# Attention logits in a decoder block: keys of the heads in place of latent queries

## The chip, the cores and the metric

The kernel runs on one core of a Trainium2 chip. The metric is the time of one execution on the device, in microseconds; the median of three runs of the kernel before is 1537.74 (1536.7 to 1537.75). Engines are named as in the profile: PE (TensorE) multiplies matrices, DVE (VectorE) and ACT (ScalarE) work on vectors, POOL is GpSimd, SP issues most DMAs.

## What is computed

A decoder block on 512 tokens of width 1024, in f32: a mixer (sparse attention beside a pooling branch, gates, an output projection, LayerNorm) and a mixture of 32 experts with four per token. The change lies in the attention. Its keys are a latent of 128 numbers per token, shared by eight heads of width 64:

```python
q_lat = jnp.einsum('bshd,rhd->bshr', q, w_uk[l]) * (ATTN_HEAD_DIM ** -0.5)
ckv = rms_norm(ckv, kv_norm_g[l])
...
logits = jnp.einsum('bqhr,bqkr->bqhk', ql, c_sel).astype(jnp.float32)
logits = logits - slopes[None, None, :, None] * dist[:, :, None, :]
p = jax.nn.softmax(logits, axis=-1).astype(c_sel.dtype)
return jnp.einsum('bqhk,bqkr->bqhr', p, c_sel)
```

A query attends only to the 128 keys that an indexer scores highest among those up to its own position. The logit of a head is a product over r (128) and d (64) of query, up-projection `w_uk` and latent; it can be bracketed from either side.

## The kernel before, in words

The program is one stream per engine, in the order in which the Python code emits it; nothing reorders it. Queries stand in four blocks of 128, and block b sees (b+1)*128 keys. The latent is kept twice: `ckv`, tokens on partitions, and `ckvT` (line 724), its 128 numbers on partitions.

The projections come first, with weights split into two parts so that three fp32r products give f32 (`proj`, line 564): 24 matmuls of 512 columns each. A pair of split weights is made three projections ahead (`one_pair`, line 536): ACT copies the high part (504 or 542), DVE subtracts it (505 or 543). A raw weight tile is free after its last split, and SP then issues the next load of its ring of four. The q projection (lines 716 to 732) also turns the latent (723), and at its third step turns the up-projection `wuk` (728) into `wukT`, scaled (729).

Scores of the indexer (`score_pair`, line 634) and rounds that take the top eight keys (`top_round`, line 654) are queued and drained between the projections, by a cost that is a formula of the number of columns (`drain`, line 664). `score_pair` multiplies two heads at a time, one on partitions 0 to 63, one on 64 to 127.

The attention (lines 907 to 923) runs eight units, (block, half of the heads), in the order of blocks 3, 0, 2, 1. `queries(b)` (line 829) makes the queries of all eight heads of a block in the latent's coordinates, 128 rows by 128 queries each, from `wukT` and `qT`, and copies them out of PSUM with DVE and ACT (837). `logits(u)` (839) multiplies four heads by `ckvT`, a head to a PSUM bank, and DVE adds the distance and the mask (849). `exponentials(u)` (853) takes the maximum (DVE, 856) and exponentiates (ACT, 858). `weights(u)` (861) divides by the sums (DVE, 867). `outputs(u)` (869) transposes the weights (877), copies them by ACT and DVE in turn (878) and multiplies by `ckv` (884); `values(u)` (887) applies `w_uv` (892). The order is set by hand:

```python
weights(u - 1)
logits(u)
outputs(u - 1)
exponentials(u)
drain(STEP_BUDGET)
if u < 7:
    ga_tile(u)
values(u - 1)
```

`queries` comes ahead of these at the units 2, 4 and 6, and once before the loop; `ga_tile` is one more projection (ACT copies it out, line 820). PSUM has four banks of tag "a" (projections and logits), two of "b" (queries, outputs, values) and two of "c" (transposes). Tiles share named slots of SBUF: a tile in a slot waits for the last reader of the tile before. After the loop come the branch products (`branch_part`, line 780), the output projection, the first norm and the router (to line 1240), and then the experts, whose weights SP loads as slots come free (`Stream`, line 183; first load in line 1038).

Of the kernel before, what the change touches and what calls it, by code (L numbers as in the profile page):

```python
# [25 lines left out]
OP = mybir.AluOpType  # L26
AX = mybir.AxisListType

P = 128
S = 512  # L30
# [4 lines left out]
HD = 64  # L35
# [35 lines left out]
def tile_hybrid_block(ctx, tc, x, c, w_ada, b_ada, w_in, kv_norm_g, w_uk, w_uv, w_pool_group,  # L71
                      pool_scale, w_branch_attn, w_branch_pool, w_out, ln1_g, ln1_b, w_router,
                      b_router, w_gate_up, b_gate_up, w_down, b_down, ln2_g, ln2_b, out):
    nc = tc.nc
# [14 lines left out]
    def bank(tag, shape=None, dt=F32):  # L89
        bufs = {"a": 4, "b": 2, "c": 2}[tag]  # L90
        return psum.tile(shape or [P, 512], dt, name="ps_" + tag, tag=tag, bufs=bufs)
# [4 lines left out]
    def slot(shape, tag, dt=F32, bufs=1, name=None):  # L96
        pool = stream if tag in LASTING else ft_last if tag in LAST else ft
        return pool.tile(shape, dt, name=name or tag, tag=tag, bufs=bufs)
# [181 lines left out]
    bada = slot([12, 512], "bada")  # L280
# [59 lines left out]
    small = {}  # L340

    def small_loads(*rows):
        def load():
            for name, shape, tag, src in rows:
                small[name] = slot(shape, tag, name=name)
                nc.sync.dma_start(small[name], src)
        return load

    feed.add("small", small_loads(("kvg", [P, R], "kvg", kv_norm_g.to_broadcast([P, R])),
                                  ("wuk", [P, 512], "u", w_uk[0].rearrange("r h d -> r (h d)")),  # L350
                                  ("wpg", [P, 4, P], "wpg", w_pool_group[0].rearrange("g c d -> c g d"))),
             ring=False)
    add_cols(("q", 0), Q0)
# [19 lines left out]
    ident = consts.tile([P, P], F32, name="ident")  # L373
# [64 lines left out]
    ps = bank("c")  # L438
# [125 lines left out]
    def proj():  # L564

        w = next_pair()
        ps = bank("a")
        proj_part(ps, w, range(KD))
        return ps
# [43 lines left out]
    def ada_group():  # L613
        g = next(ada_groups)
        ps, w = bank("c"), [ada_feed.tiles["ada2", g, j] for j in range(2)]
        for j in range(2):
            for b in range(4):
                nc.tensor.matmul(ps[32 * b:32 * b + 32, :], condp[:, 2 * (g % 4) + j, :], w[j][:, b * 512:(b + 1) * 512],
                                 start=(j == 0), stop=(j == 1))
        part = w[1][:, 0:512]  # L620
        nc.scalar.copy(part, ps)
        nc.scalar.dma_start(mod_parts[g % 4, 4 * (g // 4):4 * (g // 4) + 4, :], part[::32])
        ada_feed.mark(("ada2", g))
# [40 lines left out]
    def drain(budget):  # L664
        cost = 0.0
        if pair_q:
            b, j = pair_q.pop(0)
            cost += score_pair(b, j)
            if j == 3:
                top_q.extend((b, r) for r in range(TOPK // 8))  # L670
        while top_q and cost < budget:
            cost += top_round(*top_q.pop(0))

    BUDGET, STEP_BUDGET = 3.6, 3.0
    kiT = slot([P, S], "kiT")
# [14 lines left out]
    ckvT = slot([P, S], "ckvT")  # L690
# [3 lines left out]
    ps = bank("b", [P, NT, H])  # L694
# [5 lines left out]
    def normal_ckv():  # L700
        ps = bank("c", [P, NT, R])
        for t in range(NT):
            nc.tensor.transpose(ps[:, t, :], ckvT[:, t * P:(t + 1) * P], ident)
        for t in range(NT):
            nc.scalar.activation(sq, ps[:, t, :], AF.Square, accum_out=ssum[:, t:t + 1])
        nc.vector.tensor_scalar(ssum, ssum, 1.0 / R, EPS, op0=OP.mult, op1=OP.add)
        nc.scalar.activation(ssum, ssum, AF.Sqrt)
        nc.vector.reciprocal(ssum, ssum)
        for t in range(NT):
            nc.vector.scalar_tensor_tensor(ckv[:, t, :], ps[:, t, :], ssum[:, t:t + 1], small["kvg"],  # L710
                                           op0=OP.mult, op1=OP.mult)


    qT = slot([P, 4, S], "C0", name="qT")
    wukT = slot([P, 4, P], "bada", name="wukT")
    for j in range(4):
        nc.scalar.copy(qT[:, j, :], proj())
        if j == 0:
            normal_ckv()
        if j == 1:  # L720
            ps = bank("c")
            for t in range(NT):
                nc.tensor.transpose(ps[:, t * P:(t + 1) * P], ckv[:, t, :], ident)
            nc.scalar.copy(ckvT, ps)
        if j == 2:
            ps = bank("c")
            for i in range(4):
                nc.tensor.transpose(ps[:, i * P:(i + 1) * P], small["wuk"][:, i * P:(i + 1) * P], ident)
            nc.scalar.mul(wukT, ps.rearrange("p (j r) -> p j r", j=4), HD ** -0.5)
        if j % 2:  # L730
            ada_group()
        drain(BUDGET)
# [35 lines left out]
    for g in range(4):  # L768
        ps = proj()
# [17 lines left out]
    def branch(w, i, v):  # L787
        ps = bank("a")
        branch_part(ps, w, i, v, range(4))
        return ps  # L790

    for g in range(4):
        for i in range(2):
            n = 2 * g + i
# [10 lines left out]
        for i in range(2):  # L805
            n = 2 * g + i
# [4 lines left out]
    def selected(b):  # L811

        while any(v[0] == b for v in pair_q + top_q):
            drain(0.1)
# [4 lines left out]
    def ga_tile(n):  # L819
        nc.scalar.copy(ga[n // 4][:, n % 4, :], proj())  # L820

    ya_raw = slot([P, 4, S], "C1", name="ya_raw")
    units_at = [(b, g) for b in (3, 0, 2, 1) for g in range(2)]
    ql = [slot([P, 4, P], tag, name="ql") for tag in ("kiT", "pooled")]
    pT = slot([P, 2, 512], "usum", name="pT")
    oT = slot([P, 2, 512], "relu", name="oT")
    state = {}

    def queries(b):

        qs = slice(b * P, (b + 1) * P)
        for i in range(2):
            hp = slice(i * HD, (i + 1) * HD)
            ps = bank("b", [P, 4, P])
            for j in range(4):
                nc.tensor.matmul(ps[:, j, :], wukT[hp, j, :], qT[hp, j, qs], start=True, stop=True)
            (nc.scalar.copy if i else nc.vector.tensor_copy)(ql[i], ps)

    def logits(u):
        b, g = units_at[u]  # L840
        n = (b + 1) * P
        lg = slot([P, 4, S], f"B{u % 2}", name="lg")
        mx = slot([P, 4], "mx", bufs=2)
        sm = slot([P, 4], "sm", bufs=2)
        for i in range(4):
            h = 4 * g + i
            ps = bank("a")
            nc.tensor.matmul(ps[:, 0:n], ql[h % 2][:, h // 2, :], ckvT[:, 0:n], start=True, stop=True)
            nc.vector.scalar_tensor_tensor(lg[:, i, 0:n], dsel[b], 2.0 ** -(h + 1), ps[:, 0:n],
                                           op0=OP.mult, op1=OP.add)  # L850
        state[u] = lg, mx, sm

    def exponentials(u):
        lg, mx, sm = state[u]
        n = (units_at[u][0] + 1) * P
        nc.vector.tensor_reduce(mx, lg[:, :, 0:n], axis=AX.X, op=OP.max, negate=True)
        for i in range(4):
            nc.scalar.activation(lg[:, i, 0:n], lg[:, i, 0:n], AF.Exp, bias=mx[:, i:i + 1],
                                 accum_out=sm[:, i:i + 1])

    def weights(u):
        b, g = units_at[u]
        n = (b + 1) * P
        lg, _, sm = state[u]
        nc.vector.reciprocal(sm, sm)
        for i in range(4):
            nc.vector.tensor_scalar(lg[:, i, 0:n], lg[:, i, 0:n], sm[:, i:i + 1], None, op0=OP.mult)

    def outputs(u):
        b, g = units_at[u]  # L870
        lg = state[u][0]
        o_ps = bank("b")

        def turn(s):
            ps = bank("c")
            for i in range(4):
                nc.tensor.transpose(ps[:, i * P:(i + 1) * P], lg[:, i, s * P:(s + 1) * P], ident)
            (nc.vector.tensor_copy if s % 2 else nc.scalar.copy)(pT[:, s % 2], ps)

        turn(0)  # L880
        for s in range(b + 1):
            if s < b:
                turn(s + 1)
            nc.tensor.matmul(o_ps, ckv[:, s, :], pT[:, s % 2], start=(s == 0), stop=(s == b))
        nc.scalar.copy(oT[:, u % 2], o_ps)
# [16 lines left out]
    def mod_row(rows, r):  # L902
        ps = bank("c")
        nc.tensor.matmul(ps, pick8[:, r:r + 1].to_broadcast([40, P]), rows, start=True, stop=True)
        return ps

    queries(3)
    selected(3)
    logits(0)
    exponentials(0)  # L910
    ga_tile(0)
    for u in range(1, 8):
        if units_at[u][1] == 0:
            queries(units_at[u][0])
            selected(units_at[u][0])
        weights(u - 1)
        logits(u)
# [6 lines that stand above are left out]
# [82 lines left out]
    for n in range(KD):  # L1006
        if n < 4:
            ps = begun[n]
            branch_part(ps, wide[n // 2], n % 2, ya, range(2, 4))
        else:  # L1010
            if n % 2 == 0:
                w = next_pair()
            ps = branch(w, n % 2, ya)
# [640 lines left out]
    ps = bank("c", [P, 1, 3])  # L1654
# [80 lines left out]
    u = 3  # L1735
    while u < len(units):
        j = units[u][0]
# [8 lines left out]
        u = us[-1] + 1  # L1746

    for j in range(2, E):
        for u in units_of(j):
            p, k = max(turned[j - 1], listed.get(units.index(u), (0, 0)))  # L1750
# [28 lines left out]
    for ph in phases:  # L1779
        kind, j = ph  # L1780
# [82 lines left out]
    with tc.For_i(0, n_more, 1):  # L1863
# [11 lines left out]
        ps = [bank("a") for _ in range(4)]  # L1875
# [5 lines left out]
        ps = [bank("b") for _ in range(2)]  # L1881
# [32 lines left out]
```

## Time and profile before

| what | value |
|---|---|
| median of three runs | 1537.74 us (1536.7 to 1537.75) |
| the profiled execution | 1541.65 us |
| its span, first to last instruction | 1539.9 us |
| PE busy | 1450.7 us, 94% |
| DVE busy | 916.2 us, 59% |
| ACT busy | 626.3 us, 41% |
| POOL busy | 482.1 us, 31% |
| mean granted TensorE clock | 0.976 of full speed |

The busy shares are means over stages with different limits. Matmuls overlap each other in the records, so a stretch where PE is busy all the time is not yet one where it runs at its peak; the distance between starts is what counts. An f32 matmul stands in the trace as two records, its two passes. The times in the views run from the start of the span.

### The profile page before, as it was taken

Reading aid. Unit: us, or ns where it says so; the run is one execution under the profiler, and the core shown is the slowest. Engines: PE = TensorE matmul, PEld = TensorE weight load, DVE = VectorE, ACT = ScalarE, POOL = GpSimd, SP = SyncE. Lnnn points to the kernel's source line nnn. Section 1 sums busy time; section 2 is a strip of 40 time slices with the busy share of each in tenths; the row PEclk is TensorE's granted clock in tenths of the full one; section 3 lists DMA queues with packets and bytes.
Section 4 is the critical chain, followed back from the end, with each engine's and each line's share of the span. In section 5 each row is a group of like instructions: output and inputs, shape, how many; then the busy total and the mean of one; then the engine's idle time right before and its main releaser. Section 6 shows DMA issues by size and latency. Waiting matters only on the chain. (4 is left out here: it accounts for less than half of the span.)

```text
span 1539.9 us, 18966 instructions
## 1 busy us (share of the span) xinstructions
PE 1450.7 (94%) x6821; PEld 890.6 (58%) x6821; DVE 916.2 (59%) x1262; ACT 626.3 (41%) x725; POOL 482.1 (31%) x338
## 2 busy tenths in 40 slices
PE   7999999999979998789999999999999999999995
PEld 6766776667953332234466777534446777667551
DVE  6648878558864111034269999504416999689623
ACT  3344234452212110132257777314316676667521
POOL 2200000023531332232344444432244444434332
PEclk8999999999969999999999999999999999999998
DMA  9773530134569999999999999999999999999993
GB/s 284 248 269 134 188 120 28 57 110 192 192 223 421 407 413 407 414 407 402 346 408 414 408 368 349 366 400 408 401 341 408 414 389 344 377 408 381 363 380 138
DMA packets 106993, 489.96 MB, mean 318 GB/s; under 512 B 12513, under 2 KB 42861, under 8 KB 55696
## 3 DMA queue, kind: packets, MB, share of 16 engines
q1 hardware_dynamic: 94448, 445.25, 72.9%
q0 software_dynamic: 12304, 43.27, 9.8%
q8 instruction: 55, 0.90, 0.2%
q14 instruction: 42, 0.34, 0.1%
q10 hardware_dynamic: 144, 0.20, 0.0%
HBM read 473.36 MB, written 19.20 MB: 320 GB/s over the span
## 5 line engine op out<-in xcount | busy, mean ns | idle before, releaser
L233 DVE TENSOR_TENSOR w_lo<-raw,w_hi 128x2048 fp32r<-128x2048 f32 x168 | 422.0, 2534 | 85.3 <-ACT w_hi L224 84.8
L224 ACT ACTIVATE w_hi<-raw 128x2048 fp32r<-128x2048 f32 x168 | 320.3, 1915 | 109.0 <-PE ps_a L1399 83.3
L1409 PE MATMUL ps_a<-raw,xTn 128*64 128x512 f32 x1024 | 237.1, 606 | 12.0 <-DMA raw<-in_w_gate_up_dram 11.7
L1399 PE MATMUL ps_a<-w_hi,xT 128*128 128x512 f32 x896 | 232.6, 402 | 2.5 <-ACT w_hi L224 2.5
L1469 POOL TENSOR_TENSOR sw_l<-sw_l,sw_g 128x512 f32<-128x512 f32 x47 | 88.2, 1877 | 443.6 <-DVE sw_l L1466 295.9
L1399 PEld LDWEIGHTS ps_a<-w_hi,xT 128*128 128x128 f32 x896 | 165.5, 189 | 52.5 <-ACT w_hi L224 7.6
L1464 DVE TENSOR_SCALAR sw_g<-ps_a 128x512 f32<-128x512 f32 x46 | 31.7, 688 | 235.3 <-PE ps_a L1409 199.7
L562 PE MATMUL ps_a<-h_part,wp 128*128 128x512 f32 (+1 forms) x672 | 166.1, 402 | 3.7 <-POOL h_part L499 2.1
L1409 PEld LDWEIGHTS ps_a<-raw,xTn 128*64 128x64 f32 x1024 | 68.7, 138 | 144.5 <-issue 116.4
L562 PEld LDWEIGHTS ps_a<-h_part,wp 128*128 128x128 f32 (+1 forms) x672 | 125.0, 188 | 44.9 <-issue 11.3
L1409 PE MATMUL ps_b<-raw,aT 128*64 128x512 f32 x576 | 134.4, 601 | 9.0 <-DMA raw<-in_w_down_dram 7.2
L1399 PE MATMUL ps_a<-w_lo,xT 128*128 128x512 f32 x448 | 123.4, 398 | 4.6 <-DVE w_lo L233 4.6
L1399 PE MATMUL ps_b<-w_hi,aT 128*128 128x512 f32 x448 | 125.8, 403 | 0.0
L1399 PEld LDWEIGHTS ps_a<-w_lo,xT 128*128 128x128 f32 x448 | 84.1, 189 | 26.8 <-DVE w_lo L233 7.2
L1465 ACT ACTIVATE sw_l<-ps_a,ones 128x512 f32<-128x512 f32 x46 | 31.4, 682 | 160.8 <-PE ps_a L1409 108.8
L1399 PEld LDWEIGHTS ps_b<-w_hi,aT 128*128 128x128 f32 x448 | 81.5, 188 | 23.0 <-issue 6.2
L1409 PEld LDWEIGHTS ps_b<-raw,aT 128*64 128x64 f32 x576 | 37.0, 136 | 82.2 <-issue 59.6
L1470 POOL TENSOR_TENSOR sw_l<-sw_l,xg 128x512 f32<-128x512 f32 x47 | 75.2, 1600 | 3.7
L1500 POOL TENSOR_TENSOR yn<-yn,gate 64x512 f32<-64x512 f32 x30 | 46.1, 1536 | 92.7 <-ACT yn L1494 50.2
L1399 PE MATMUL ps_b<-w_lo,aT 128*128 128x512 f32 x224 | 70.9, 398 | 1.6 <-DVE w_lo L233 1.6
L1378 POOL DMA_INDIRECT xg<-h_rows,sl_wr x33 | 55.2, 1672 | 26.0 <-PE ps_c L1336 10.0
L505 DVE TENSOR_TENSOR wp<-raw,wp 128x1024 fp32r<-128x1024 f32 x29 | 37.7, 1311 | 26.3 <-ACT wp L504 26.2
(400 smaller groups left out, 1916.1 us busy)
## 6 DMA issues: line engine op xcount, KB each, us to landing
raw<-in_w_gate_up_dram SPq DMA_DIRECT2D x256, 1024.0 KB, 15.2
raw<-in_w_down_dram SPq DMA_DIRECT2D x128, 1024.0 KB, 11.8
ada<-in_w_ada_dram POOLq DMA_DIRECT2D x16, 1024.0 KB, 5.3
raw<-in_w_in_dram SPq DMA_DIRECT2D x14, 1024.0 KB, 9.0
raw<-in_w_ada_dram SPq DMA_DIRECT2D x32, 256.0 KB, 6.0
raw<-in_w_out_dram SPq DMA_DIRECT2D x4, 1024.0 KB, 5.4
x<-in_x_dram SPq DMA_DIRECT2D x8, 256.0 KB, 7.6
raw<-in_w_branch_pool_dram SPq DMA_DIRECT2D x2, 1024.0 KB, 5.6
```

What stands on the lines that cost most here:

```text
L224: nc.scalar.activation(c["hi"], c["w"], AF.Copy)
L233: nc.vector.tensor_sub(c["lo"], c["w"], c["hi"].bitcast(F32))
L505: eng.tensor_sub(pair[:, 1], view, pair[:, 0].bitcast(F32))
L562: nc.tensor.matmul(ps, w[:, part, k, :], h(k), start=(k == part == 0 and h is hh), stop=(k == last and h is hl))
L1378: nc.gpsimd.indirect_dma_start(out=v, out_offset=None, in_=in_halves if narrow else h2_rows[:, :], in_offset=bass.IndirectOffsetOnAxis(ap= ...
L1399: nc.tensor.matmul(ps[i], a[:, part, k + j, :], m[:, cs], start=first and j == 0 and part == 1, stop=last and j == 4 // n - 1 and m is lo)
L1409: nc.tensor.matmul(ps[i][h * 64:(h + 1) * 64], a[:, kk, c * 64:(c + 1) * 64], w["w"][:, cs], start=first and j == 0, stop=last and j == 4 ...
L1464: nc.vector.tensor_scalar(g, ps[i], LIMIT, None, op0=OP.min)
L1465: nc.scalar.activation(l, ps[len(ps) // 2 + i], AF.Identity, bias=ones[:, 0:1])
L1469: eng.tensor_mul(l, l, g)
L1470: eng.tensor_mul(l, l, sig)
L1500: nc.gpsimd.tensor_mul(y[rows], y[rows], gate2[rows, h * 512:(h + 1) * 512])
```

## The change

The up-projection is no longer turned. Its tile lies in another slot, and before the first unit it is multiplied by the latent: four products, each the keys of two heads over 512 tokens, one head on partitions 0 to 63 and one on 64 to 127. DVE and ACT read them out in turn, with the scale. The keys take the slots of the two tiles of latent queries, of the pooling input `up`, and of `ckvT` itself. The logits multiply a head's 64 rows of `qT` by its 64 rows of keys. `queries` is gone.

```diff
@@ -347,7 +347,7 @@
-                                  ("wuk", [P, 512], "u", w_uk[0].rearrange("r h d -> r (h d)")),
+                                  ("wuk", [P, 512], "bada", w_uk[0].rearrange("r h d -> r (h d)")),
@@ -712,7 +712,6 @@
     qT = slot([P, 4, S], "C0", name="qT")
-    wukT = slot([P, 4, P], "bada", name="wukT")
@@ -722,11 +721,6 @@
-        if j == 2:
-            ps = bank("c")
-            for i in range(4):
-                nc.tensor.transpose(ps[:, i * P:(i + 1) * P], small["wuk"][:, i * P:(i + 1) * P], ident)
-            nc.scalar.mul(wukT, ps.rearrange("p (j r) -> p j r", j=4), HD ** -0.5)
@@ -821,20 +815,22 @@
-    ql = [slot([P, 4, P], tag, name="ql") for tag in ("kiT", "pooled")]
...
-    def queries(b):
-
-        qs = slice(b * P, (b + 1) * P)
-        for i in range(2):
-            hp = slice(i * HD, (i + 1) * HD)
-            ps = bank("b", [P, 4, P])
-            for j in range(4):
-                nc.tensor.matmul(ps[:, j, :], wukT[hp, j, :], qT[hp, j, qs], start=True, stop=True)
-            (nc.scalar.copy if i else nc.vector.tensor_copy)(ql[i], ps)
+    keys = []
+
+    def head_keys():
+
+        for j, tag in enumerate(("kiT", "pooled", "u", "ckvT")):
+            ps = bank("b")
+            nc.tensor.matmul(ps, small["wuk"][:, j * P:(j + 1) * P], ckvT, start=True, stop=True)
+            keys.append(slot([P, S], tag, name="keys"))
+            if j % 2:
+                nc.scalar.mul(keys[j], ps, HD ** -0.5)
+            else:
+                nc.vector.tensor_scalar(keys[j], ps, HD ** -0.5, None, op0=OP.mult)
@@ -845,7 +841,8 @@
-            nc.tensor.matmul(ps[:, 0:n], ql[h % 2][:, h // 2, :], ckvT[:, 0:n], start=True, stop=True)
+            hp = slice(h % 2 * HD, (h % 2 + 1) * HD)
+            nc.tensor.matmul(ps[:, 0:n], qT[hp, h // 2, b * P:(b + 1) * P], keys[h // 2][hp, 0:n], start=True, stop=True)
@@ -904,14 +901,13 @@
-    queries(3)
+    head_keys()
     selected(3)
...
         if units_at[u][1] == 0:
-            queries(units_at[u][0])
             selected(units_at[u][0])
```

## Rows read from the trace of the kernel before

**Rows 1.** Busy by stretch: stretch, then us busy of each engine, granted clock, DMA share, GB/s.

```profile
216.00:240.00 24.00, 22.44 (x88) 13.27 (x87) 15.92 (x24) 7.98 (x15) 0.00 (x0) 1.00 0.13 43
430.00:450.00 20.00, 14.54 (x73) 13.33 (x74) 11.56 (x26) 2.09 (x4) 8.00 (x8) 0.50 0.33 119
```

**Rows 2.** Timeline of PE, q projection and indexer: start, us, engine, line, form, records.

```profile
88.85 1.13 PE L639 MATMUL ps_b<-kiT,qiT 64*128 64x512 f32 x4
89.91 5.76 PE L562 MATMUL ps_a<-h_part,wp 128*128 128x512 f32 x24
95.51 0.60 PE L728 MATMUL ps_c<-ident,wuk 128*128 128x128 f32 x4
96.04 1.13 PE L639 MATMUL ps_b<-kiT,qiT 64*128 64x512 f32 x4
...
146.47 0.70 PE L639 MATMUL ps_b<-kiT,qiT 64*128 64x256 f32 x4
147.10 5.75 PE L562 MATMUL ps_a<-h_part,wp 128*128 128x512 f32 x24
```

**Rows 3.** Timeline of PE in the attention; in brackets idle time and what ended it.

```profile
216.65 1.71 PE L836 MATMUL ps_b<-qT,wukT 64*128 64x128 f32 x16
219.05 3.67 PE L848 MATMUL ps_a<-ckvT,ql 128*128 128x512 f32 x8 [0.69 <-ACT ql L837]
222.16 6.04 PE L562 MATMUL ps_a<-h_part,wp 128*128 128x512 f32 x24
228.03 3.60 PE L848 MATMUL ps_a<-ckvT,ql 128*128 128x512 f32 x8
231.70 1.86 PE L877 MATMUL ps_c<-ident,lg 128*128 128x128 f32 x8
...
245.26 1.71 PE L836 MATMUL ps_b<-qT,wukT 64*128 64x128 f32 x16
247.21 1.38 PE L848 MATMUL ps_a<-ckvT,ql 128*128 128x128 f32 x8 [0.23 <-DVE ql L837]
...
260.83 1.16 PE L848 MATMUL ps_a<-ckvT,ql 128*128 128x128 f32 x8
261.83 0.60 PE L877 MATMUL ps_c<-ident,lg 128*128 128x128 f32 x4
...
272.20 2.85 PE L848 MATMUL ps_a<-ckvT,ql 128*128 128x384 f32 x8 [0.23 <-DVE ql L837]
274.89 0.60 PE L877 MATMUL ps_c<-ident,lg 128*128 128x128 f32 x4
...
298.72 2.01 PE L848 MATMUL ps_a<-ckvT,ql 128*128 128x256 f32 x8 [0.23 <-DVE ql L837]
300.56 1.04 PE L877 MATMUL ps_c<-ident,lg 128*128 128x128 f32 x8
```

**Rows 4.** Timeline of DVE, steps 0 to 2 of the attention.

```profile
218.22 0.68 DVE L837 COPY ql<-ps_b 128x512 f32<-128x512 f32 x1
220.19 0.69 DVE L849 SCALAR_TENSOR_TENSOR lg<-dsel,ps_a 128x512 f32<-128x512 f32 x1 [1.28 <-PE ps_a L848]
221.04 0.69 DVE L849 SCALAR_TENSOR_TENSOR lg<-dsel,ps_a 128x512 f32<-128x512 f32 x1 [0.17 <-PE ps_a L848]
...
223.48 2.29 DVE L856 TENSOR_REDUCE mx<-lg 128x4 f32<-128x2048 f32 x1
...
232.65 2.48 DVE L849 SCALAR_TENSOR_TENSOR lg<-dsel,ps_a 128x512 f32<-128x512 f32 x4
...
246.46 0.69 DVE L837 COPY ql<-ps_b 128x512 f32<-128x512 f32 x1 [0.26 <-PE ps_b L836]
```

**Rows 5.** Timeline of DVE, step 6.

```profile
297.97 0.69 DVE L837 COPY ql<-ps_b 128x512 f32<-128x512 f32 x1 [1.96 <-PE ps_b L836]
...
300.11 1.41 DVE L849 SCALAR_TENSOR_TENSOR lg<-dsel,ps_a 128x256 f32<-128x256 f32 x4
```

**Rows 6.** SP's DMAs: the up-projection (start in us), and the first expert weights (timeline).

```profile
L346 SPq DMA_DIRECT2D wuk<-in_w_uk_dram x1: 430/430/430, 44.3 to 44.3; - x1
...
348.27 0.33 SPq L139 DMA_DIRECT2D raw<-in_w_gate_up_dram  x1
```

## The prediction

> **What bounds the kernel now.** I read the busy shares by stretch first, then TensorE's timeline, then VectorE's. Between 216 and 240 us, where the attention begins, TensorE is busy 22.44 of 24 us at a granted clock of 1.00, VectorE 15.92 of 24, and the DMA engines 0.13 [rows 1]. So no transfer bounds this stage; the question at each step is whether TensorE or the chain VectorE, ScalarE, VectorE comes last.
>
> The stage is a loop of eight units (block, half of the heads), in order of blocks 3, 3, 0, 0, 2, 2, 1, 1. Step u divides unit u-1 by its sums (VectorE, line 867), makes the logits of u (848, 849), turns and sums u-1 (877, 884), and runs a gate projection (562) and the values (892). In [rows 3], what matters is the distance from one start to the next, since busy times overlap. Two things are to be seen there. The 16 records of the queries (836) delay the logits by 245.26 to 247.21 = 1.95 us, ahead of blocks 0, 2 and 1 alike (three times; the first takes 2.40, to 219.05). And the logits of four heads take 272.20 to 274.89 = 2.69 at 384 keys, 1.84 at 256 (298.72 to 300.56), 1.00 at 128 (260.83 to 261.83): two passes for a head, one after the other.
>
> Who comes last differs. At step 6 VectorE stands idle 1.96 us until the queries are done [rows 5]: TensorE bounds. At step 1 and 2 it is VectorE: its reduction (856) of unit 0 starts at 223.48, and all that leads to the first transposes at 231.70 hangs on it; at step 2 it waits 0.26 for the queries and copies them for 0.69 before it can go on with the division [rows 4].
>
> **Removed: four transposes of the up-projection** and a ScalarE copy, in the q projection. Start to start they take 96.04 - 95.51 = 0.53 [rows 2]. TensorE runs without a gap there, so I take **-0.5**; the bounds are 0 (if the split weights then come late) and -0.53.
>
> **Moved: where that weight lies.** Its load, one DMA on the SyncE queue at 44.3 us [rows 6], now goes to the slot of the small bias tile, whose readers are four transposes of the first microseconds. The queue waits for nothing new, no DMA is added, and POOL's clearing of the pooling tile's edge loses a wait. Cost nothing.
>
> **Added: keys of the heads.** Four products of 512 columns. One costs 221.04 - 220.19 = 0.86, the pace of the logits before [rows 4]. Two PSUM buffers serve them, so the third waits until VectorE has read the first: VectorE is free at 218.22 and needs 0.68, until 218.90, where the third was due at 216.65 + 1.71 = 218.36. That is a new wait of 0.54, with the fourth product and the first logits queued behind it. The logits start at 216.65 + 3.44 + 0.54 = 220.63 instead of 219.05. The second and fourth eviction lie on ScalarE, which is idle. Bounds of the new wait: 0 to 0.68.
>
> **Changed: logits.** Contraction over 64 rows instead of 128, neighbouring heads in different row groups. The trace has the very form: the indexer's pairs (line 639, 64 rows, two heads, two passes each) take 89.91 - 88.85 = 1.06 at 512 columns and 147.10 - 146.47 = 0.63 at 256 [rows 2]. Four records of 512 one after the other would take 1.72. So a pair costs two passes, 0.21 us per 128 columns, plus an edge of about 0.2. Two pairs in a row, if the edge falls once, give 1.91, 1.49, 1.06 and 0.63 us for 512, 384, 256 and 128 keys; with an edge each, 0.21 more. I take the first, since the heads follow each other without a change of shape, and keep 0.21 per unit as bound.
>
> **Steps 0 to 2.** Unit 0's logits start 1.58 later, but two heads arrive at once: after some 1.2 us (before, 220.19 - 219.05 = 1.14 for one), at 221.85. VectorE then needs four evictions back to back, as at 232.65, where four take 2.48 [rows 4], a pace of 0.60. It is through at 224.3, so the reduction starts **+0.8** late, and with it the exponentials, the weight split and the first transposes. What step 1 gains in its own logits is lost: TensorE waits for the division. At step 2 VectorE drops the wait and the copy of the queries, 0.26 + 0.69: **-0.95**. TensorE is ready earlier still, so the division decides, and the stage stands at -0.15 there. Bounds: +0.8 to -0.95.
>
> **Steps 3 to 7**, TensorE's own sums: step 3, 1.00 - 0.63 = 0.37; step 4, queries 1.95 and logits 2.69 - 1.49 = 1.20; step 5, 1.20 again (same shape); step 6, 1.95 and 1.84 - 1.06 = 0.78; step 7, 0.78. Together **-8.2**. The VectorE copy of the queries goes with them. What is late next is VectorE's four evictions of each unit, but TensorE turns the unit before meanwhile, and the banks come back before the next projection.
>
> **Sum**: -0.5 - 0.15 - 8.2 = **-8.9 us**. Behind it, everything starts from the last values of the attention; the first expert weights are asked for at 348.27 [rows 6], by a queue that waits for freed slots, so the expert stage should move as a whole. The profiled execution took 1541.65 us (span 1539.9), 3.9 over the median of 1537.74; I put the gain on the median: **1528.8**. The bounds above, added, give -9.7 to -5.5, that is 1528.0 to 1532.2.
>
> **Rivals.**
>
> Evictions pace the logits. Two heads at once leave VectorE four evictions that take 2.48 at 512 and 1.41 at 256 keys [rows 4, 5], by the same step 1.95 at 384 and 0.88 at 128. If the transposes had to wait for these, steps 3 to 7 would give 0.12, 2.69, 0.74, 2.38 and 0.43, in all 6.4 instead of 8.2: 1530.7. Against it: no bank and no tile ties the transposes of u-1 to the evictions of u. The Trainium skill, TensorEngine Tiling (Array Packing), section PSUM Bottleneck, says that tiling speeds up TensorE but not the emptying of PSUM, which may then bound. By that rule the sum is this rival's; the trace agrees where VectorE is the late one (step 1). Chance 0.10.
>
> The pairs don't run side by side, as the change says they do. Then only the queries of steps 4 and 6 are saved, 3.9, and the transposes' 0.5, against 1.58 - 0.95 = 0.6 lost at the start: -3.8, 1533.9. Against it stands the indexer's 1.06. Chance 0.05.
>
> The gain is swallowed behind the attention, by a later stage that is held by something which doesn't move: 1537.7. For it: later stages have their own waits, and in 430 to 450 us TensorE is granted 0.50 and busy only 14.54 of 20 [rows 1]. Against: I find no transfer or timer there that isn't released by the attention's work. Chance 0.13.
>
> Slower: the clock falls inside the attention. It stands at 1.00 in 216:240 and at 0.50, the 1.2 GHz level, in 430:450, where TensorE waits often [rows 1]. The place is the wait ahead of the first transposes (231.70), which grows by 0.8 plus what the logits of step 1 save, with half of the array used before it. If the clock fell there and stayed down until step 3's transposes (261.83), 30 us would do the work of 15: +15, 1543.8. It decides from about 18 us at half clock, which eat 8.9. Against it: the wait is some 2.5 us (228.03 + 1.91 to 232.5), and projections of nearly 6 us lie on either side (222.16 to 228.03) [rows 3]. Chance 0.06.
>
> **Numbers.** The forecast has 0.66. Faster by over 0.2% (3.1 us, about what a measurement can tell from no change) is the forecast and the first two rivals: 0.81; same 0.13; slower 0.06. The range goes from 1526.5 (the bound of 1528.0, and some of the later half-clock stretches gone with the shift) to 1534.6, which takes in both smaller gains and leaves out the last two rivals, 0.19.
>
> **What would show it.** Right: logits in 1.9, 1.5, 1.1 and 0.6 us per four heads, two records starting together; no queries; the reduction of unit 0 some 0.8 late against the start of the stage, step 2's transposes level with before, the last values about 8.4 earlier against it, and the first expert load 8.9 earlier on the span's clock. Wrong: logits that keep 0.86 per head; transposes from step 3 on that wait for VectorE; a granted clock below 1.00 before 326 us; or an attention that ends 9 us earlier and an expert stage that starts where it did.

## The result and the profile after

The changed kernel takes 1531.59 us (median of six runs, 1525.95 to 1532.72), the kernel before beside it 1537.74 (six runs, 1536.7 to 1540.08). The ratio is 0.995, with an interval of 0.9938 to 0.9962, that is 5.8 to 9.5 us less; the medians differ by 6.15. The profiled execution took 1532.72, its span is 1530.9. The prediction was 1528.8, from 1526.5 to 1534.6: faster is right, the size was too large: 8.9 for 6.15 by the medians, while the ratio of 0.995 stands for 7.7.

The page's busy times come first; they answer to the table of before.

```profile
PE 1439.7 (94%) x6761; PEld 877.8 (57%) x6761; DVE 911.4 (60%) x1260; ACT 624.4 (41%) x722; POOL 480.5 (31%) x338
```

TensorE works 11.0 us less, VectorE 4.8 less. The attention itself, TensorE's timeline of the changed kernel (start, us, engine, line, form, records, idle time before and what ended it):

```profile
213.48 1.88 PE L828 MATMUL ps_b<-ckvT,wuk 128*128 128x512 f32 x4
215.87 1.98 PE L828 MATMUL ps_b<-ckvT,wuk 128*128 128x512 f32 x4 [0.52 <-DVE keys L833]
217.79 1.99 PE L845 MATMUL ps_a<-keys,qT 64*128 64x512 f32 x8
219.71 5.73 PE L562 MATMUL ps_a<-h_part,wp 128*128 128x512 f32 x24
225.37 1.98 PE L845 MATMUL ps_a<-keys,qT 64*128 64x512 f32 x6
228.19 1.12 PE L845 MATMUL ps_a<-keys,qT 64*128 64x512 f32 x2 [0.84 <-ACT ga L814]
229.68 1.86 PE L874 MATMUL ps_c<-ident,lg 128*128 128x128 f32 x8 [0.37 <-DVE lg L864]
...
258.89 0.71 PE L845 MATMUL ps_a<-keys,qT 64*128 64x128 f32 x8
259.54 0.66 PE L874 MATMUL ps_c<-ident,lg 128*128 128x128 f32 x4
...
268.03 1.56 PE L845 MATMUL ps_a<-keys,qT 64*128 64x384 f32 x8
269.52 0.66 PE L874 MATMUL ps_c<-ident,lg 128*128 128x128 f32 x4
...
290.32 1.13 PE L845 MATMUL ps_a<-keys,qT 64*128 64x256 f32 x8
291.38 1.09 PE L874 MATMUL ps_c<-ident,lg 128*128 128x128 f32 x8
...
313.44 1.03 PE L874 MATMUL ps_c<-ident,lg 128*128 128x128 f32 x8
```

Read it against [rows 3], start to start. The logits of four heads take 217.79 to 219.71 = 1.92 us at 512 keys, 1.49 at 384, 1.06 at 256 and 0.65 at 128, where the forecast had 1.91, 1.49, 1.06 and 0.63; before they took 2.69, 1.84 and 1.00 at 384, 256 and 128. No queries stand ahead of them. The third key product waits 0.52 us for VectorE, where the forecast had 0.54. But the logits of unit 0 start 217.79 - 213.48 = 4.31 after the stage does, against 3.98 forecast, and TensorE now stands idle twice at step 1: for 0.84 us ahead of the last head's logits, until ScalarE has read out a bank (line 814), and for 0.37 ahead of the first transposes, until VectorE has divided (line 864). Before, it went from the logits to the transposes without a stop (228.03 + 3.60 against 231.70, [rows 3]).

VectorE's timeline shows why the first reduction, and all that hangs on it, is late, and what does not bound the later steps:

```profile
215.14 0.68 DVE L833 TENSOR_SCALAR keys<-ps_b 128x512 f32<-128x512 f32 x1
...
218.95 2.48 DVE L846 SCALAR_TENSOR_TENSOR lg<-dsel,ps_a 128x512 f32<-128x512 f32 x4 [1.22 <-PE ps_a L845]
221.47 2.29 DVE L853 TENSOR_REDUCE mx<-lg 128x4 f32<-128x2048 f32 x1
...
291.05 1.42 DVE L846 SCALAR_TENSOR_TENSOR lg<-dsel,ps_a 128x256 f32<-128x256 f32 x4
```

The four evictions of unit 0 go back to back in 2.48 us, as forecast, and the reduction starts 221.47 - 213.48 = 7.99 after the stage's start; before it was 223.48 - 216.65 = 6.83 [rows 3, 4]. At step 6 the evictions run from 291.05 to 292.47, while TensorE turns the unit before from 291.38 on and waits for nothing there.

One thing was forecast at 1.00 throughout and is not. The stretches of the changed kernel (us busy of PE, PEld, DVE, ACT, POOL, then the granted clock, DMA share and GB/s):

```profile
230.00:232.00 2.00, 1.57 (x8) 0.95 (x9) 2.00 (x5) 0.58 (x1) 0.00 (x0) 1.00 0.00 0
232.00:234.00 2.00, 2.00 (x5) 0.92 (x6) 1.71 (x3) 0.00 (x0) 0.00 (x0) 0.53 0.00 0
234.00:236.00 2.00, 2.00 (x8) 1.03 (x6) 0.00 (x0) 0.59 (x1) 0.00 (x0) 0.61 0.00 0
```

For some 4 us behind the wait the clock is below 1.00 and falls to near 0.5, the 1.2 GHz level. This is called a dip below. Before, [rows 1] have 1.00 over the whole of 216 to 240.

Ahead of the stage, the removed transposes show as a shorter distance between the q projection and the indexer's next product, and behind it the first expert weights are asked for earlier:

```profile
87.27 5.76 PE L562 MATMUL ps_a<-h_part,wp 128*128 128x512 f32 x24
92.95 1.13 PE L639 MATMUL ps_b<-kiT,qiT 64*128 64x512 f32 x4
```

```profile
338.43 6.24 SPq L139 DMA_DIRECT2D raw<-in_w_gate_up_dram  x2
```

The first is TensorE's timeline, the second SyncE's. 92.95 - 87.27 = 5.68 against 96.04 - 89.91 = 6.13 [rows 2]: 0.45 less. The first expert load comes 9.84 us earlier than before (348.27, [rows 6]). Not all of that is the change: the profiled execution of before was already 2.64 us later at the q projection (89.91 against 87.27), behind work that is the same in both kernels; at 20 to 30 us its clock was granted 0.69, the other's 0.97. That is why the rest of this document measures the stage from its own start, and repeats both kernels.

### The profile page after: what moved, and what is told of

The parts are those of the page before. It is cut to its first block, busy times and chain, and to the rows that moved or that the text cites. A ratio compares the mean times of both kernels' runs of the same rounds, so it can differ in the third digit from the quotient of the medians.

```text
span 1530.9 us, 18841 instructions
## 1 busy us (share of the span) xinstructions
PE 1439.7 (94%) x6761; PEld 877.8 (57%) x6761; DVE 911.4 (60%) x1260; ACT 624.4 (41%) x722; POOL 480.5 (31%) x338
```

## The experiments

Three questions were open. Is the low clock a course of one execution or a consequence of the new wait? Which parts gave and cost what the sum says? And can the loss at steps 0 and 1 be had back? The shares below are taken from the first product of the stage (line 828 after, 836 before) to three places: the first values of step 1, the values of step 2, and the last transposes, those of unit 7 (in the changed kernel of above 313.44 - 213.48 = 99.96).

### Both kernels once more

**The changed kernel, no edit.** 

> The changed kernel once more, for a second profile. Theory (the start of the program differs from execution to execution, and the change is worth what its own stage shows): measured against the start of the attention, the first transposes come 1.1 us later than in the kernel before and the steps 3 to 7 give 7.9; the first 50 us may differ from the first profile by up to 3 us either way; the granted clock dips below 1.00 between the first transposes and the second output product again, about 1 us. Rival (the start belongs to the change): the first 50 us are 2.6 us shorter than in the kernel before, again. Rival (the dip is chance): 1.00 throughout the attention, and an attention 1 us shorter than in the first profile. Time: 1529 to 1532.

**The kernel before, no edit.** 

> The kernel before once more, for a second profile. Theory (what the two first profiles differ by outside the attention is the course of single executions): no dip of the clock in the attention; the q projection to the attention's start as in the first profile; the first 50 us shorter than in the first profile by 1 to 3 us, since all four profiles of kernels with the change were so by 0.9 to 2.9; span 1535 to 1538; ratio 1.000 within its interval. Rival (the change shortens the start): the first 50 us as in the first profile within 0.5.

The repeated kernel before took 1539.48 us, ratio 1.0002 (0.999 to 1.0013) against 1540.08. The repeated change took 1532.18 (1530.65 to 1534.04) against 1538.36, ratio 0.9963 (0.995 to 0.9977). Its clock is 1.00 all through 205 to 330 us: the dip that was expected didn't come. Nor does the shorter start belong to the change: the indexer's first product (line 639) stands at 78.84 us in the repeated kernel before (79.82 in its first profile, 0.98 more) and at 78.88 in the repeated change (77.17 in its first). TensorE's timeline of the kernel before, repeated, and behind it of the change, repeated:

```profile
215.68 1.71 PE L836 MATMUL ps_b<-qT,wukT 64*128 64x128 f32 x16
...
232.87 1.12 PE L884 MATMUL ps_b<-pT,ckv 128*128 128x512 f32 x2 [0.29 <-ACT pT L878]
...
249.07 1.13 PE L884 MATMUL ps_b<-pT,ckv 128*128 128x512 f32 x2 [0.29 <-ACT pT L878]
...
322.25 1.03 PE L877 MATMUL ps_c<-ident,lg 128*128 128x128 f32 x8
```

```profile
215.19 1.88 PE L828 MATMUL ps_b<-ckvT,wuk 128*128 128x512 f32 x4
...
233.54 1.12 PE L881 MATMUL ps_b<-pT,ckv 128*128 128x512 f32 x2 [0.29 <-ACT pT L875]
...
248.79 1.12 PE L881 MATMUL ps_b<-pT,ckv 128*128 128x512 f32 x2 [0.29 <-ACT pT L875]
...
314.09 1.03 PE L874 MATMUL ps_c<-ident,lg 128*128 128x128 f32 x8
```

From the stage's start, the first values stand at 17.19 before and 18.35 after: **+1.16**, where +0.8 was forecast. The values of step 2 stand at 33.39 and 33.60: +0.21, so step 2 gave back 0.95, as forecast. The last transposes stand at 106.57 and 98.90: -7.67, so steps 3 to 7 gave 7.88 of the 8.2. The stage without a dip thus gains 7.67.

### Two more of the change, and the wait filled

The longer idle time at step 1 (0.84 us) is filled with products that feed nothing:

```diff
         weights(u - 1)
+        if u == 1:
+            keep_warm(6)
         logits(u)
```

> The changed kernel with six 128-column products of the identity, which nobody reads, ahead of the logits of unit 1, so that TensorE works where it waited for ScalarE and VectorE. Theory (the wait lets the clock fall, which costs 1 us): 1.00 throughout the attention, the span from the first logits to the values of unit 0 about 1.0 us shorter, time 1.0 less than the changed kernel. Rival (the dip is chance or comes from somewhere else): the dip stays, or it is absent in the unfilled kernel too; same time. Rival (the fill delays what VectorE waits for): first transposes later by up to 1.3, time 0.5 to 1.3 more.

> The changed kernel, a third profile. So far the clock dipped below 1.00 in the attention in two of the four profiles that have TensorE's wait ahead of the first transposes (the changed kernel once of two, the order 0, 2, 1, 3 once, the added products not), and in none of the four in which that wait is filled or gone. Theory (the wait makes the dip possible, and the course of the execution decides): a dip between 225 and 255 us in at least one of this and the fourth profile, where it costs 1 to 2 us. Rival (the dip came with the first profile alone and has nothing to do with the wait): none in both.

> The changed kernel, a fourth profile. Theory (the wait makes the dip possible): a granted clock below 1.00 between 225 and 255 us in at least one of the third and the fourth profile. Rival: none in both.

> The kernel with the wait filled by products that nobody reads, a second profile. Theory: 1.00 from 205 to 326 us. Rival (the dip has nothing to do with the wait): a dip here too.

The filled kernel takes 1532.7 us, ratio 0.9959 (0.9945 to 0.9972): the same as the change, so the 1.0 us less that was expected is not seen in the time. The single executions of the later three took 1532.86 and 1533.93 us (change) and 1531.93 (filled). In its first profile TensorE has 12 records more (line 580) and the first transposes come no later, 230.75 - 214.55 = 16.20 after the stage's start, as in the change (229.68 - 213.48 = 16.20); the 0.84 is gone, the 0.37 stays:

```profile
226.35 1.50 PE L580 MATMUL ps_c<-ident 128*128 128x128 f32 x12
...
230.75 1.86 PE L874 MATMUL ps_c<-ident,lg 128*128 128x128 f32 x8 [0.37 <-DVE lg L864]
```

The third profile of the change, busy by stretch, has the dip twice:

```profile
234.00:236.00 2.00, 2.00 (x5) 0.86 (x5) 1.44 (x3) 0.00 (x0) 0.00 (x0) 0.50 0.00 0
...
250.00:252.00 2.00, 2.00 (x6) 1.04 (x5) 0.05 (x1) 0.00 (x0) 0.00 (x0) 0.50 0.55 213
```

In the fourth profile the clock is below 1.00 in 232 to 238 us, with 0.50 in the middle. From the stage's start to the last transposes the four profiles of the change take 99.96, 98.90, 101.39 and 99.92 us; the two of the filled kernel 98.93 and 98.92, at a clock of 1.00. Against 98.90 a dip costs 1.1 and 1.0, and 2.5 where it comes twice in one execution. Over all profiles: the dip stands in four of the six whose first transposes wait as in the change (the order of heads and the added queries below are the other two: with and without it), and in none of the seven where that wait is filled, shorter or absent (before twice, filled twice, split keys twice, one row group once). The change against the filled kernel alone is three of four against none of two. That the wait opens the door to the dip is likely by this count, and not shown beyond it; in which executions the clock then falls, these profiles don't tell. The mean stage of the change is 100.04, 1.1 over the stage without a dip. In the timed medians this 1.1 can't be seen: the intervals are some 4 us wide.

### The order of the heads

```diff
-        for i in range(4):
+        for i in (0, 2, 1, 3):
```

The heads of one row group now follow each other in twos. 

> The changed kernel with the heads of a unit multiplied in the order 0, 2, 1, 3, so that neighbours stand in the same row group. Theory (two heads run side by side only when the next one in order stands in the other row group): four heads take about 3.0, 2.3, 1.5 and 0.8 us for 512, 384, 256 and 128 keys instead of 1.9, 1.5, 1.1 and 0.65; steps 3 to 7 give 2.6 us less; time 2 to 3 us above the changed kernel. Rival (the row groups keep queues of their own, and order does not matter): the same durations and the same time. Rival (it is the 64 rows that are faster, not the two side by side): the same.

It took 1532.73 us, ratio 0.9966 (0.9954 to 0.9978). TensorE's timeline:

```profile
218.05 1.99 PE L845 MATMUL ps_a<-keys,qT 64*128 64x512 f32 x8
219.98 5.73 PE L562 MATMUL ps_a<-h_part,wp 128*128 128x512 f32 x24
...
270.03 1.57 PE L845 MATMUL ps_a<-keys,qT 64*128 64x384 f32 x8
271.53 0.66 PE L874 MATMUL ps_c<-ident,lg 128*128 128x128 f32 x4
```

1.93 and 1.50, as in the natural order. The expectation that the pairs must be neighbours in the program fell. VectorE's timeline shows what does change:

```profile
219.21 0.69 DVE L846 SCALAR_TENSOR_TENSOR lg<-dsel,ps_a 128x512 f32<-128x512 f32 x1 [1.22 <-PE ps_a L845]
220.07 1.88 DVE L846 SCALAR_TENSOR_TENSOR lg<-dsel,ps_a 128x512 f32<-128x512 f32 x3 [0.17 <-PE ps_a L845]
```

The second head in the program, of the same row group as the first, is ready only 0.86 us after it, the pace of one head behind the other; the last three are then evicted back to back. So each row group seems to work through its own heads in order, beside the other group. The reduction starts 221.99 - 213.74 = 8.25 after the stage does, 0.26 later than in the natural order (7.99). The profile had the dip twice (0.50 in 232:234 and again in 250:252), and its stage took 315.47 - 213.74 = 101.73 us, 2.8 more than without: these 0.26 and some 2.5 for two dips.

### One row group for all heads

```diff
-            hp = slice(h % 2 * HD, (h % 2 + 1) * HD)
+            hp = slice(0, HD)
```

Odd heads take the queries and keys of the even ones; the work of the stage stays the same in size, the attention's values don't. 

> The changed kernel with all heads multiplied from the first 64 rows, so the odd heads take queries and keys of the even ones; shapes and counts stay. Theory (two heads run side by side because they stand in different row groups): four heads take 3.5, 2.7, 1.8 and 1.0 us, as with 128 rows, steps 3 to 7 give 4.2 us less, first transposes no later than 0.5; time 4 to 5 us above the changed kernel. Rival (a product over 64 rows is the faster one, whatever rows): 1.9, 1.5, 1.1 and 0.65, same time.

The whole took 1739.91 us, ratio 1.1307, far above what was expected. That is no price of the logits: 205 us of it lie behind the last transposes (1738.1 - 318.43 = 1419.7, in the repeated change 1528.8 - 314.09 = 1214.7). This trace has 1024 expert products into one buffer (line 1395, `ps_a<-w_hi,xT`) in place of 896, the last at 1674 us, which fits a router that, with other values, sends tokens to other experts. Only the stage can be read, on TensorE's timeline:

```profile
218.30 3.70 PE L845 MATMUL ps_a<-keys,qT 64*128 64x512 f32 x8
221.93 5.73 PE L562 MATMUL ps_a<-h_part,wp 128*128 128x512 f32 x24
...
268.70 2.84 PE L845 MATMUL ps_a<-keys,qT 64*128 64x384 f32 x8
271.48 0.66 PE L874 MATMUL ps_c<-ident,lg 128*128 128x128 f32 x4
...
318.43 1.04 PE L874 MATMUL ps_c<-ident,lg 128*128 128x128 f32 x8
```

3.63 us at 512 keys and 2.78 at 384, against 1.92 and 1.49: the pace of one head after the other. The stage takes 318.43 - 213.99 = 104.44, **5.54 more** than the repeated change. Of the 7.67 that the stage gains, the row groups side by side bring 5.5.

### The queries put back as dead weight

```diff
         if units_at[u][1] == 0:
+            for i in range(2):
+                hp = slice(i * HD, (i + 1) * HD)
+                ps = bank("b", [P, 4, P])
+                for j in range(4):
+                    nc.tensor.matmul(ps[:, j, :], keys[j][hp, 0:P], qT[hp, j, 0:P], start=True, stop=True)
```

Eight products in the form of the queries, whose results nobody reads or copies. 

> The changed kernel with eight products over 64 rows of 128 columns again ahead of the units 2, 4 and 6, in the form of the queries, read by nobody and without their copies. Theory (TensorE bounds from step 3 on, VectorE at step 2): the one at unit 2 costs nothing up to 0.3 us, those at units 4 and 6 cost their 1.4 us in full each; 2.9 us in all, time 2 to 3.5 above the changed kernel. Rival (the wait for the copies, 0.5 of the 1.95, was what counted and the products were cheap): under 1 us in all. Rival (VectorE bounds all steps): nothing at any of the three.

It took 1534.17 us, ratio 0.9973 (0.9962 to 0.9983). TensorE's timeline:

```profile
246.10 0.37 PE L845 MATMUL ps_a<-keys,qT 64*128 64x128 f32 x1
246.20 0.27 PE L915 MATMUL ps_b<-qT,keys 64*128 64x128 f32 x1
...
248.84 1.12 PE L881 MATMUL ps_b<-pT,ckv 128*128 128x512 f32 x2 [0.29 <-ACT pT L875]
...
273.07 1.12 PE L881 MATMUL ps_b<-pT,ckv 128*128 128x512 f32 x2 [0.73 <-ACT pT L875]
...
296.36 1.12 PE L881 MATMUL ps_b<-pT,ckv 128*128 128x512 f32 x2 [0.29 <-ACT pT L875]
```

Measured from its stage's start at 215.23, the values of step 2 stand at 33.61, in the repeated change at 33.60: at step 2 the products cost **nothing**, since VectorE's division is late there (in the repeated change the transposes of step 2 wait 0.89 us for line 864). At step 4 the values stand 1.46 later than in the repeated change (57.84 against 56.38), at step 6 another 1.45 (81.13 against 78.22). The same instructions are free at one step and cost nearly their whole time at the next two. The first two rows show a logits record (845) that starts ahead of a dead-weight record (915), though all dead-weight records stand ahead of these logits in the program. The time does not confirm the 2 to 3.5 us that were expected: the ratio lies 0.0010 above the repeated change's, 1.5 us, and the intervals are 3 to 4 us wide, so the 2.9 of the stage is not excluded either.

### Keys in two halves

Unit 0 needs the keys of four heads. The products for the other four go behind its logits, and ScalarE evicts all but one:

```diff
-    head_keys()
+    head_keys((0, 1))
     selected(3)
     logits(0)
+    head_keys((2, 3))
...
-            if j % 2:
+            if j != 1:
```

> The changed kernel with only the keys of heads 0 to 3 made ahead of the first logits, the others right behind them, and ScalarE reading out all but the second. Theory (the chain VectorE, ScalarE, VectorE from the first logits to the first transposes is what ends last until step 2, and the four products ahead of it cost their whole 3.4 us plus the wait for a bank): against the start of the attention the first logits on VectorE come 2.2 us earlier than in the changed kernel, the first transposes 2 to 2.4 earlier, no dip of the clock there (1 us more), steps 3 to 7 as before; time 2.5 to 3.5 us below the changed kernel. Rival (TensorE bounds there): four products stay four products, time the same within 0.5.

It took 1528.34 us (1526.46 to 1529.14), ratio 0.9933 (0.992 to 0.9947); its slowest run lies below the fastest of the repeated change on the same chip (1530.65). **It beats both kernels.** TensorE's timeline:

```profile
213.20 1.88 PE L829 MATMUL ps_b<-ckvT,wuk 128*128 128x512 f32 x4
215.01 1.99 PE L846 MATMUL ps_a<-keys,qT 64*128 64x512 f32 x8
216.93 1.98 PE L829 MATMUL ps_b<-ckvT,wuk 128*128 128x512 f32 x4
218.35 6.04 PE L562 MATMUL ps_a<-h_part,wp 128*128 128x512 f32 x24
...
229.05 1.12 PE L882 MATMUL ps_b<-pT,ckv 128*128 128x512 f32 x2 [0.29 <-ACT pT L876]
...
309.60 1.03 PE L875 MATMUL ps_c<-ident,lg 128*128 128x128 f32 x8
```

The logits start 1.81 after the stage instead of 4.31, no product waits for a bank, and the first values stand at 15.85 instead of 18.35. All of these 2.50 us reach the end of the stage: 309.60 - 213.20 = 96.40 against 98.90. Step 2 now waits as long as ever for the division, so what is gained ahead of unit 0's reduction is gained whole. Its clock has no dip; these 2.50 and the 1.1 that dips cost the change on the mean make 3.6, where the medians differ by 3.8.

### And the selection's rounds moved

At step 2 VectorE comes last, behind rounds of the selection that `drain` gave it at step 1. They are put off to later steps:

```diff
-        drain(STEP_BUDGET)
+        drain({1: 0.0, 4: 2.0, 5: 2.0}.get(u, STEP_BUDGET))
```

> The kernel with half of the keys ahead of the first logits, and with the five selection rounds of step 1 moved to later steps (none at step 1, up to five at 2 and 3, up to three at 4 and 5). Theory (at step 2 VectorE is last because of these rounds): the division of unit 1 starts about 0.8 us earlier against the stage's start, then behind ScalarE's split of the weights and no longer behind rounds; step 2's second group of transposes 0.8 to 1.2 earlier, all later steps keep that; time 0.5 to 1.2 below the kernel with half of the keys first. Rival (the rounds come back as a wait at steps 4 or 6): the same time or up to 1 more.

With the split keys it took 1528.75 us (1524.94 to 1530.23), ratio 0.9931 (0.9916 to 0.9945). TensorE's timeline:

```profile
243.84 1.95 PE L875 MATMUL ps_c<-ident,lg 128*128 128x128 f32 x8 [0.16 <-DVE lg L865]
```

Of the five rounds that step 1 had, one now runs at step 3, three at step 4 and one at step 5. The wait ahead of the transposes of step 2 falls from 0.91 (split keys) to 0.16, and the stage to 311.39 - 215.72 = 95.67, 0.73 less than with the split keys alone. In the time that can't be told from the split keys, where 0.5 to 1.2 less was expected.

## Why the prediction was right and where it was wrong

**Right, by its own steps.** The range took in both smaller gains, so that the time lies in it says little of the mechanism, and the median of 1531.59 is nearer to the 1530.7 of the rival in which the evictions pace the logits than to 1528.8; the rows decide. The pairs: 1.92, 1.49, 1.06 and 0.65 us, with the edge falling once for two pairs, as chosen. (What the forecast calls the two passes of a product are its two records; what TensorE does in one no run shows.) The one-row-group run shows that the row groups are the cause. The queries: dead weight put back costs 1.46 and 1.45 at steps 4 and 6 and nothing at step 2, which is what the sum said of who comes last there; it is less than the 1.95 of before: there is no copy to wait for (0.23 idle ahead of the logits in [rows 3]), and some of their records run beside the first logits. The new bank wait: 0.52 for 0.54. Step 2: 0.95 for 0.95. The transposes: 0.45 for 0.5, inside the bounds; over the whole way from the indexer's first product to the stage's start it is 0.52 (136.83 and 136.84 us before, 136.30 or 136.31 in every profile with the change).

**Wrong: the step "It is through at 224.3, so the reduction starts +0.8 late".** It is 1.16 (7.99 - 6.83 from the rows, and the same at the first values). Two terms were too small, and 0.85 (224.33 - 223.48) had been rounded to 0.8. The eviction of the first keys starts 215.14 - 213.48 = 1.66 after the stage does, behind a round of the selection, where 218.22 - 216.65 = 1.57 was read from before; the third product so starts at 2.39 and not at 2.25. And the pair of products behind the wait takes 215.87 to 217.79 = 1.92, where 2 x 0.86 = 1.72 was taken: by the starts of the records 0.2 more on the way from 128-row products to 64-row ones, where the forecast had an edge in the logits only. With the keys in two halves the same pair, without a wait in front, takes 213.20 to 215.01 = 1.81, so about half of the 0.2 may belong to the start behind the wait; these runs don't part the two.

**Wrong by a little: steps 3 to 7,** 7.88 for 8.2. The values of the steps stand 0.29, 3.07, 1.14, 2.67 and 0.71 earlier (repeated change against repeated before), each 0.06 to 0.08 less than forecast. The rows of steps 3, 4 and 6 show most of it: the transposes behind the 64-row logits have 0.66, 0.66 and 1.09 in place of 0.60, 0.60 and 1.04 [rows 3], an edge again.

**Wrong: "I put the gain on the median" with a clock of 1.00.** Corrected for the terms above, the sum is 0.52 + 7.67 = 8.2. A clock below 1.00 before 326 us was on the forecast's own list of signs against it, and it came. The rival of the falling clock had the right place, the wait ahead of the first transposes, and the wrong price: it gave 30 us at half clock and 15 us, and the runs show some 4 us at a time, once or twice, for 1.0 to 2.5 us in all, in four profiles of six. With the mean of the four profiles of the change (a stage of 100.04, 6.5 less than the repeated before) the sum is 6.5 + 0.5 = 7.0. The medians say 6.15 and 6.18, with intervals of 5.8 to 9.5 and of 0.0023 x 1538.36 = 3.5 to 0.005 x 1538.36 = 7.7: 7.0 lies in both, 8.9 in the first alone. The ratios, 0.995 and 0.9963, stand for 7.7 and 5.7, one on either side of 7.0. The 0.8 between 7.0 and the medians these runs can't settle. Two executions of the same kernel differ by more: the stage of the change starts at 213.48 in one profile and between 215.19 and 215.21 in the other three, and its clock in 20 to 30 us goes from 0.60 to 0.97.

**The other rivals.** Evictions that pace the logits: 6.4 for steps 3 to 7 was its price, 7.88 was measured, and no transpose of these steps waits for them. The rule of the Trainium skill, TensorEngine Tiling (Array Packing), section PSUM Bottleneck, that the emptying of PSUM gains nothing from tiling and may then bound, holds in this trace at one place, the start of unit 0, where VectorE's four evictions take 2.48 us against 1.92 for the products. Pairs that don't overlap: refuted by the rows and by the run with one row group. A gain swallowed behind the attention: the first expert load comes 24.96 to 25.00 us after the last transposes in every profile, and from the last transposes to the end of the span it takes 1216.6 and 1216.5 us before and 1213.8 to 1217.5 in the ten profiles with the change that keep the attention's values. So nothing behind takes the gain back, though single executions differ there by 3.7. The change and every timed version of it that leaves the attention's values as they are lie below the kernel before, too.

## What to carry to other kernels

Price an instruction by who comes last at its step, not by its duration: the same eight products cost 0 at one step and some 1.45 at each of the next two steps that have them. Where a product is made once in place of many times, make only what the first reader needs ahead of it and the rest behind: here that was worth 2.5 us of the stage, and 1532.18 - 1528.34 = 3.8 of the median. A faster TensorE ahead of a chain on another engine turns into idle time, and, as the count of dips makes likely, idle time on TensorE can cost clock behind it; several profiles of a kernel that fills it are the way to tell.

## What was not expected of the hardware

The heads needn't alternate between the row groups in the program: in the order 0, 2, 1, 3 four heads of 512 keys take 1.93 us, as in the order 0, 1, 2, 3 (1.92), and in the run with dead weight a logits record starts at 246.10 us ahead of a record at 246.20 that stands before it in the program. An order with all heads of one group first was not tried.

The change of contraction height has an edge of its own: by the records' starts 0.1 us (no wait in front) or 0.2 (behind a wait) from 128-row products to 64-row ones, and 0.05 from these to the transposes. The first is rough: with the keys in two halves, two 128-row products behind the logits take only 216.93 to 218.35 = 1.42, less than the 1.72 of their four records, so a start can be placed too early.

The clock can fall after a short wait (0.84 and 0.37 us idle), in some executions and not in others of one kernel; it is then below 1.00 in two or three stretches of 2 us in a row. The wait of 0.89 to 0.91 us ahead of step 2's transposes, which eight profiles have, was followed by a dip in two of them, and both had dipped at step 1.
